# A pool that outlives the head for the second half's first weights, constants and first query block, and a product taken in turn with its transpositions

## The chip, the core and the metric

The kernel runs on one core of a Trainium2 chip. The core has five engines with an instruction queue each: TensorE (PE in the profile, with its weight loads as PEld), VectorE (DVE), ScalarE (ACT), GpSimd (POOL) and SyncE (SP). SP computes nothing here; it issues nearly all DMA transfers, one after the other, and an instruction that has to wait holds up everything behind it on its queue. PE multiplies matrices and also transposes 128 x 128 blocks (a multiplication by the identity, `c_ident`); it writes to PSUM only, and ACT or DVE copy ("evacuate") its results to SBUF. The metric is the time of one execution on the chip, in microseconds (us); less is better. Times of the profile are counted from the start of its span.

## What is computed

One layer of a transformer on 1024 tokens of width 1024, all in float32: a hybrid attention block, a cross attention to a memory of 256 rows, and a squared-ReLU MLP, each with a root-mean-square norm ahead and a residual sum behind. Only the start of the attention block matters here. Cut to that:

```python
proj = h @ w_in                                   # h: normed x, w_in: 1024 x 1760
c_q, c_kv, k_idx, w_idx, q_nsa, kv_nsa, g_nsa = split(proj)
c_q, c_kv = rms_norm(c_q, dsa_cq_g), rms_norm(c_kv, dsa_ckv_g)
q_d = rope(rms_norm(c_q @ w_dsa_uq))              # dense-sparse attention, 8 heads of 64
q_i = rope(c_q @ w_idx_q)                         # indexer: picks 256 keys for each query
q_n = rope(rms_norm(q_nsa))                       # three-branch attention, 8 heads of 64
k_c = rope(rms_norm(compress(kv_nsa[:, :, 0])))   # 63 compressed keys; v_c likewise
...
for each block of 128 queries:
    indexer scores and top 256; attention over them; compressed, selected and window attention
```

## The kernel before

Tokens are worked on in tiles of 128. `project(pool, part, late, st)` (L410) does everything up to queries and keys, for four tiles at a time: part 0 is the head of the program (its pool is `p1`, its PSUM tags D, M and C), part 1 the second half (pool `p2`, opened when `p1` is closed). A part transposes the normed x into `xh` (`to_T`, L294), multiplies it with chunks of 256 columns of `w_in` (`gemm`, L342, whose matmuls all stand at L233), and handles each result in `consume` (L461). In the head the float32 operands are split into a high and a low part (`whi`, `wlo`, L261 and L266: two engines make them from `wraw`); in the second half each weight is used whole and the two tags are only two rings of buffers (`load_whole`, L278). The first chunk is columns 968 to 1224, the raw keys and values of the compressed branch; its result is doubled by ACT (L487), transposed by PE (L490) and copied to `c8` tiles.

The x tiles of the second half are loaded in the head and normed in place by `norm_ahead` (L400). At the start of part 1 they are transposed (eight 128 x 128 blocks a tile, in two PSUM buffers of four, evacuated by ACT at L306 or DVE at L308), and then come, in the code's order, eleven small loads of constants into two `pc` tiles (L437 to L447: gains of norms, and cosine and sine rows that DVE multiplies at L441 and L442), the loads of the first weights, and the first product. At that moment p1 has just been closed, the main PSUM pool has been opened (two buffers for D, one for M, two each for S and PT), and the attention of the first half begins beside part 1: `q_prep` (L613) loads a block of 128 queries by 4 heads from DRAM into `qin` (one buffer), ACT squares it (L627), DVE reduces it (L629), POOL takes the root and normalizes (L630 to L632), POOL and DVE apply the rotation (L633 to L637), and PE transposes it (L643) into a PT buffer. The queries lie in DRAM since the head (`qraw`, written from `st` by `stage_q`, L459).

`together` (L123) and `attend` (L885) interleave attention and the rest in the code; the final order on each engine is made by a scheduler of the framework, which takes the instructions by priority as its own model of time lets them start. A tile in a pool has a tag with a number of buffers; a new tile of the tag waits until an old one is no longer used. With `reuse_waits="tile"` a pool that opens over the memory of a closed one waits tile by tile for what lay there.

Of the kernel before, what the change touches and what calls it, by code (L numbers as in the profile page):

```python
# [9 lines left out]
F32 = mybir.dt.float32  # L10
# [12 lines left out]
P = 128  # L23
# [11 lines left out]
NS = 4  # L35
G = 3
RINGS = {
    "p1": {"x4": 5, "st": 2, "relu": 4, "wraw": 4, "whi": 6, "wlo": 6, "c8": 4, "c4": 2, "kraw": 5, "pc": 2},
    "p2": {"x4": 5, "st": 2, "relu": 2, "whi": 4, "wlo": 4, "c8": 3, "c4": 1, "kraw": 4, "pc": 2},
    "dn": {"b4": 4, "h": 8, "relu": 2, "wraw": 2, "whi": 4, "wlo": 4},  # L40
    "res": {"b4": 4, "g": 2},
    "d2": {"b4": 4, "xo": 2, "h": 8, "relu": 4, "wraw": 6, "whi": 8, "wlo": 8},
# [137 lines left out]
def build(nc, tc, I, C, out):  # L180
# [8 lines left out]
    at = at_pool.__enter__()  # L189
    sp_pool = tc.tile_pool(name="sp", bufs=1, side="right", reuse_waits="tile")  # L190
    srow = sp_pool.__enter__()
    p1_pool, p1_psum = tc.tile_pool(name="p1", bufs=1, reuse_waits="tile"), tc.tile_pool(name="ps1", bufs=1, space=PSUM)
    p1 = p1_pool.__enter__()
    psum.update(pool=p1_psum.__enter__(), n=PSUMS["p1"])
# [205 lines left out]
    def norm_ahead(pool):  # L400

        gb = gain(pool, W["norm1_g"])
        for t in range(4, 8):
# [3 lines left out]
            v.scalar_tensor_tensor(ahead[t], ahead[t], r[:, 0:1], gb, op0=ALU.mult, op1=ALU.mult)  # L407
            yield 1.0

    def project(pool, part, late, st):  # L410
        t0, nt = PARTS[part]
        whole = part > 0
# [9 lines left out]
                load_x(ahead[t], t)  # L422
            begun += list(ws)
        for t in range(nt):
            if whole:
                to_T(pool, ahead.pop(t0 + t), xt_of(t), DM // P, ("M", "D", "D"))
            else:
                norm_T(pool, ahead.pop(t), gb1, xt_of(t))
            yield 1.0
        pe = late["pe"]  # L430
        cq = [ring(pool, "c8", [P, nt, 2, P], F32 if whole else F32R) for _ in xf]
        ckv = [ring(pool, "c4", [P, nt, P], F32 if whole else F32R) for _ in xf]
        kraw = [ring(pool, "kraw", [P, 6, 64]) for t in range(nt)]
        KT = []
        pc = ring(pool, "pc", [P, 512])
        cqg, ckvg, ctab = pc[:, 0:256], pc[:, 256:384], pc[:, 384:512].rearrange("p (a d) -> p a d", d=64)
        nc.sync.dma_start(cqg, row(W["dsa_cq_g"]).to_broadcast([P, 256]))  # L437
        nc.sync.dma_start(ckvg, row(W["dsa_ckv_g"]).to_broadcast([P, 128]))
        nc.sync.dma_start(ctab[:, 0, :], C["c_ccos"])
        nc.sync.dma_start(ctab[:, 1, :], C["c_csin"])  # L440
        v.tensor_tensor(ctab[:, 0, :], ctab[:, 0, :], qg[:, 2, :], op=ALU.mult)  # L441
        v.tensor_tensor(ctab[:, 1, :], ctab[:, 1, :], qgs[:, 2, :], op=ALU.mult)  # L442
        kg = ring(pool, "pc", [P, 8, 64])
        lnb = kg[:, 6, :]
        for h, src in enumerate([W["nsa_kn_g"][1:2], W["nsa_kn_g"][1:2], W["nsa_kn_g"][2:3], W["nsa_kn_g"][2:3],
                                 row(W["dsa_kn_g"]), row(W["idx_k_ln_g"]), row(W["idx_k_ln_b"])]):
            nc.sync.dma_start(kg[:, h, :], src.to_broadcast([P, 64]))  # L447

        qst = []

# [89 lines left out]
        for kv in range(0 if part else 2):  # L540
            p3 = pe[:, kv, :].rearrange("p (a l) -> p a l", a=2)
            g.tensor_copy(KT[kv][0:64, :, nt * P:], p3[0:64])
            g.tensor_copy(KT[kv][64:128, :, nt * P:nt * P + 15], p3[64:128, :, 1:])
        yield from w_in([[(968, 256)]], 4, begun)
        yield from w_in([[(0, 256)], [(256, 200), (1736, 24)]], 0)
        pair_ = (w_in([[(1224, 256)], [(1480, 256)]], 5), compress(pool, part, KT, pe, st, ctab))
        yield from (alternate if part == 0 else chain)(*pair_)
        yield from gemm(pool, [lambda t, k, c=c: c[:, t, :] for c in ckv], 1, nt,
                        W["w_dsa_ukv"], [[(0, 128)]], consume_kv)
        yield from alternate(w_in([[(456, 256)], [(712, 256)]], 2), k_prep())  # L550
        ups = chain(*[gemm(pool, [lambda t, k, c=c: c[:, t, k, :] for c in cq], 2, nt,
                           W[name], [[(0, 256)], [(256, 256)]],
                           lambda ci, t, pt, k=k: stage_q(k, ci, t, pt)) for k, name in ((0, "w_dsa_uq"), (2, "w_idx_q"))])
# [58 lines left out]

    def q_prep(aw, t, kind, hg):  # L613

        q = small(aw, "qin", 256, bufs=1).rearrange("p (h d) -> p h d", d=64)
        part = part_of(t)
        nc.sync.dma_start(q, qraw[kind][part][hg][:, t - PARTS[part][0], :].rearrange("p (h d) -> p h d", d=64))
        ta = small(aw, "qta", 256, bufs=1).rearrange("p (h d) -> p h d", d=64)
        tb = small(aw, "qtb", 256, bufs=1).rearrange("p (h d) -> p h d", d=64)
        if kind == 2:  # L620
            A, B = cos[:, t, None, None, :].to_broadcast([P, 4, 2, 32]), sin[:, t, :]
        else:
            tab = small(aw, "qtab", 128, bufs=1).rearrange("p (a d) -> p a d", d=64)
            g.tensor_tensor(halves(tab[:, 0, :]), halves(qg[:, kind, :]), cos[:, t, None, :].to_broadcast([P, 2, 32]), op=ALU.mult)
            g.tensor_tensor(tab[:, 1, :], sin[:, t, :], qgs[:, kind, :], op=ALU.mult)
            A, B = halves(tab[:, 0, :])[:, None, :, :].to_broadcast([P, 4, 2, 32]), tab[:, 1, :]
            s.activation(ta, q, AF.Square)  # L627
            ss, r = small(aw, "qss", 4), small(aw, "qr", 4)
            v.tensor_reduce(ss, ta, axis=AX.X, op=ALU.add)  # L629
            g.tensor_scalar(ss, ss, 64 * EPS, None, op0=ALU.add)  # L630
            g.tensor_tensor(r, ss, mhalf[:, 0:1].to_broadcast([P, 4]), op=ALU.pow)
            g.tensor_tensor(q, q, r[:, :, None].to_broadcast([P, 4, 64]), op=ALU.mult)  # L632
        g.tensor_tensor(halves(ta), halves(q), A, op=ALU.mult)  # L633
        v.tensor_tensor(halves(tb), swap(q), halves(B)[:, None, :, :].to_broadcast([P, 4, 2, 32]), op=ALU.mult)
        qd = small(aw, "qd", 512, bufs=1).rearrange("p (h b d) -> p h b d", h=4, b=2)
        v.tensor_tensor(qd[:, :, 0, :], ta, tb, op=ALU.add)
        g.tensor_tensor(qd[:, :, 1, :], ta, tb, op=ALU.add)  # L637
        own = ("iqh", "iql", 1) if kind == 2 else ("qh", "ql", 2)
        qh = aw.tile([P, 4, P], F32R, tag=own[0], name=own[0], bufs=own[2])
        ql = aw.tile([P, 4, P], F32R, tag=own[1], name=own[1], bufs=own[2])  # L640
        p2 = pst("PT", [P, 4, P])
        for h in range(4):
            te.transpose(p2[:, h, :], qd[:, h, :, :].rearrange("p b d -> p (b d)"), ident)  # L643
        split_ps(p2, qh, ql)
        return qh, ql
# [683 lines left out]
    def fill():  # L1329
        for part in range(1, len(PARTS)):  # L1330
            with tc.tile_pool(name="p2", bufs=1, reuse_waits="tile") as p2:
                yield from project(p2, part, late, st)
            projected.append(part)
        dn = dn_pool.__enter__()
        yield from memory(dn)
        yield 1, PACES[1]
        yield from between(dn, 0, 2, {}, False)
        yield 3, PACES[2]
        x2s, made = {}, {}
        yield from between(dn, 2, 2, x2s, True, None, lambda: pre_norms(dn, made, x2s))  # L1340
        yield 3, PACES[3]
        yield from mlp(dn, 0, 4, x2s, made)
        yield 5, PACES[4]
        rows = dn.tile([P, 2, 8 * 256], F32, tag="xh", name="xh")
        room = [rows[:, 0, :].rearrange("p (t k n) -> p t k n", t=2, k=8),
                dn.tile([P, 2, 8, 256], F32, tag="xl", name="xl"), rows[:, 1, :].rearrange("p (k n) -> p k n", k=8)]
        yield from between(dn, 4, 2, late["x2s"], False, None, None, room)
# [47 lines left out]
```

## Time and profile before

| | us |
|---|---|
| median of 3 runs | 1745.03 (1742.69 to 1746.1) |
| the profiled execution | 1746.53 |
| its span | 1744.8 |
| mean granted clock of PE over the span | 0.977 of full speed |

The profiled execution is 1.5 us above the median. In the profile's lists a row reads: start, duration, engine, line of the kernel, operation, output<-input, shapes, count, and in brackets how long the engine sat idle before and what ended that. Rows by stretch read: the stretch, its length, busy time and number of instructions of PE, PEld, DVE, ACT and POOL, then PE's granted clock, the share of time in which the 16 DMA engines were busy, and GB/s. Busy shares are means over stages with different limits; what counts is which wait ends last at the place in question.

### The profile page before, as it was taken

How to read it: one execution, taken by the hardware profiler on the slowest of the kernel's cores; microseconds unless marked ns; L12 is line 12 of the kernel's file. 1: busy time of each engine (PE TensorE's matmuls, PEld its weight loads, DVE VectorE, ACT ScalarE, POOL GpSimd, SP SyncE). 2: the span in 40 equal slices, each digit the busy share in tenths (PEclk: the TensorE clock that was granted, in tenths of full speed). 3: DMA queues.
4: the chain of work that ended last, by engine and by line, in shares of the span. 5: the costliest groups of instructions: out<-in, count | busy, mean ns of one | idle time of the engine just before them, and what ended most of it. 6: DMA issues, size and time to landing. Idle time of an engine off the chain costs nothing.

```text
span 1744.8 us, 28298 instructions
## 1 busy us (share of the span) xinstructions
PE 1650.8 (95%) x9390; PEld 1444.2 (83%) x9390; DVE 1006.7 (58%) x2404; ACT 1096.8 (63%) x2749; POOL 938.2 (54%) x1091
## 2 busy tenths in 40 slices
PE   6998998899999998999999999999989899999999
PEld 6997987789878887888888888888878787888888
DVE  4564668767775885666547655555445644333344
ACT  4443796994689689857995589954345554333344
POOL 2354556564552545585676675754153565444455
PEclk9998999999999999999999999999989899999999
DMA  7335222546335312122222122126383444333354
GB/s 206 118 129 121 70 62 70 191 125 174 96 97 182 90 50 64 49 79 73 63 76 78 59 69 74 61 70 224 121 280 99 130 144 122 97 97 97 97 166 136
DMA packets 169521, 192.22 MB, mean 110 GB/s; under 512 B 24608, under 2 KB 134944, under 8 KB 169376
## 3 DMA queue, kind: packets, MB, share of 16 engines
q1 hardware_dynamic: 161296, 179.42, 33.5%
q0 software_dynamic: 7936, 10.49, 2.3%
q8 instruction: 74, 1.21, 0.3%
q14 instruction: 71, 0.58, 0.1%
q10 hardware_dynamic: 144, 0.52, 0.1%
HBM read 172.56 MB, written 17.83 MB: 109 GB/s over the span
## 4 chain that ended last, share of the span: by engine, by line
PE 65%; DVE 9%; POOL 7%; ACT 7%; issue 6%; DMA 5%; SPq 1%; POOLq 0%; ACTq 0%; DVEq 0%
PE psD L233 35%; PE psS L233 16%; PE psM L233 5%; PE psPV L233 4%; PE psPT L753 4%; POOL wlo L266 2%; ACT dmask L697 2%; DMA wraw<-in_w_ff_in_dram 2%; PE psM L302 1%; POOL S L743 1%; ACT S L738 1%; DVE pl L253 1%; DVE S L736 1%; ACT whi L261 1%; PE psPT L643 1%
## 5 line engine op out<-in xcount | busy, mean ns | idle before, releaser
L266 POOL TENSOR_TENSOR wlo<-wraw,whi 128x512 fp32r<-128x512 f32 (+1 forms) x249 | 341.5, 1378 | 251.1 <-ACT whi L261 245.3
L261 ACT ACTIVATE whi<-wraw 128x512 fp32r<-128x512 f32 x369 | 228.3, 627 | 219.2 <-PE psD L233 119.0
L233 PE MATMUL psD<-whi,h 128*128 128x512 f32 x688 | 237.6, 398 | 2.1 <-DVE b L1252 2.0
L266 DVE TENSOR_TENSOR wlo<-wraw,whi 128x512 fp32r<-128x512 f32 (+1 forms) x120 | 125.6, 1049 | 157.5 <-ACT whi L261 120.6
L253 DVE TENSOR_TENSOR pl<-psPT,ph 128x512 fp32r<-128x512 f32 (+1 forms) x232 | 141.8, 620 | 65.4 <-ACT ph L252 64.4
L233 PE MATMUL psD<-wlo,xh 128*128 128x256 f32 (+1 forms) x640 | 176.2, 352 | 1.8 <-DMA wlo<-in_w_in_dram 1.8
L738 ACT ACTIVATE S<-S,mn 128x128 f32<-128x128 f32 (+7 forms) x192 | 142.8, 744 | 54.3 <-DVE mn L736 52.4
L233 PE MATMUL psD<-whi,xh 128*128 128x256 f32 (+1 forms) x640 | 173.8, 351 | 0.9 <-DVE Vd L253 0.9
L252 ACT ACTIVATE ph<-psPT 128x512 fp32r<-128x512 f32 (+1 forms) x232 | 122.4, 540 | 63.8 <-PE psPT L753 55.2
L743 POOL TENSOR_SCALAR S<-S,sums,gi 128x640 f32<-128x640 f32 (+7 forms) x128 | 109.8, 867 | 88.5 <-DVE sums L741 69.5
L233 PEld LDWEIGHTS psD<-whi,h 128*128 128x128 f32 x688 | 129.5, 189 | 28.1 <-DVE b L1252 2.6
L753 PE MATMUL psPT<-c_ident,S 128*128 128x128 f32 x816 | 134.7, 277 | 10.1 <-POOL S L743 3.4
L233 PE MATMUL psD<-wlo,h 128*128 128x512 f32 x344 | 136.9, 399 | 0.1
L233 PEld LDWEIGHTS psD<-wlo,xh 128*128 128x128 f32 x640 | 121.6, 195 | 11.2 <-issue 1.9
L233 PEld LDWEIGHTS psD<-whi,xh 128*128 128x128 f32 x640 | 119.8, 195 | 9.5 <-DVE Vd L253 1.1
L233 PE MATMUL psD<-xh,whi 128*128 128x512 f32 (+1 forms) x352 | 124.1, 353 | 1.0 <-ACT whi L261 1.0
L233 PE MATMUL psD<-xh,wlo 128*128 128x512 f32 (+1 forms) x352 | 122.9, 349 | 0.0
L233 PE MATMUL psD<-xl,whi 128*128 128x512 f32 (+1 forms) x352 | 122.6, 349 | 0.0
L233 PE MATMUL psS<-K,qh 128*128 128x384 f32 (+3 forms) x288 | 111.3, 390 | 8.6 <-ACT ir L665 3.2
L753 PEld LDWEIGHTS psPT<-c_ident,S 128*128 128x128 f32 x816 | 99.1, 142 | 21.9 <-POOL S L743 7.4
L233 PE MATMUL psS<-K,ql 128*128 128x384 f32 (+3 forms) x288 | 97.0, 342 | 0.0
L743 POOL TENSOR_SCALAR S<-S,sums 128x128 f32<-128x128 f32 (+7 forms) x64 | 48.2, 767 | 77.8 <-DVE sums L741 55.2
(333 smaller groups left out, 4577.1 us busy)
## 6 DMA issues: line engine op xcount, KB each, us to landing
wraw<-in_w_ff_in_dram SPq DMA_DIRECT2D x44, 512.0 KB, 4.0
wraw<-in_w_ff_out_dram SPq DMA_DIRECT2D x44, 512.0 KB, 4.1
wraw<-in_w_ff_in_dram SPq DMA_DIRECT2D x64, 256.0 KB, 2.8
wraw<-in_w_ff_out_dram SPq DMA_DIRECT2D x64, 256.0 KB, 2.7
wraw<-in_w_in_dram SPq DMA_DIRECT2D x24, 256.0 KB, 3.6
q<-st SPq DMA_DIRECT2D x12, 512.0 KB, 2.8
qin<-q SPq DMA_DIRECT2D x44, 128.0 KB, 2.4
whi<-in_w_out_dram SPq DMA_DIRECT2D x20, 256.0 KB, 3.4
```

What stands on the lines that cost most here:

```text
L233: te.matmul(o, a, b, start=start, stop=stop)
L252: s.activation(hi, src, AF.Copy)
L253: v.tensor_tensor(lo, src, hi, op=ALU.subtract)
L261: s.activation(hi, raw, AF.Copy)
L266: (v if l == "v" else g).tensor_tensor(lo, raw, hi, op=ALU.subtract)
L302: te.transpose(pt[:, j, :], x_t[:, (c + j) * P:(c + j + 1) * P], ident)
L643: te.transpose(p2[:, h, :], qd[:, h, :, :].rearrange("p b d -> p (b d)"), ident)
L697: s.activation(mask, src, AF.Sign, bias=c, accum_out=over)
L736: v.tensor_tensor_reduce(out=dst, in0=sp, in1=m, scale=1.0, scalar=mn[:, 0:1] if i else 3e38, op0=ALU.add, op1=ALU.min, accum_out=low)
L738: s.activation(S, S, AF.Exp, bias=low, scale=-1.0, accum_out=sums[:, hh:hh + 1])
L743: g.tensor_scalar(Ss[hh], Ss[hh], sums[:, hh:hh + 1], 1.0 if gate is None else gate[:, hh:hh + 1], op0=ALU.mult, op1=ALU.mult)
L753: te.transpose(p2[:, j, hh, :], S[:, (c + j) * P:(c + j + 1) * P], ident)
```

## The change

A new pool `pre` is opened below `p1` and closed only when part 1 is done. Into it the head loads, ahead of its own key preparation, the four weight tiles of the second half's first product (`late["first"]`, 1 MB) and a second set of constants (`late["small"]`; the loads and DVE's two products have become the function `constants`). After the key preparation it loads the first query block (`late["q"]`) from the DRAM buffer that was written just before. `q_prep` uses that tile for the first block, and has two `qin` buffers instead of one for all others. In part 1 the transpositions of tile t+1 now stand, in the code, ahead of the first product's group for tile t, and they alternate over the tags M and D instead of M, D, D. The `pc` tag is gone from p1's and p2's rings.

```diff
+    pre_pool = tc.tile_pool(name="pre", bufs=1, reuse_waits="tile")
+    pre = pre_pool.__enter__()
     p1_pool, p1_psum = tc.tile_pool(name="p1", bufs=1, reuse_waits="tile"), tc.tile_pool(name="ps1", bufs=1, space=PSUM)
...
+    def constants(pool):
+        pc, kg = [pool.tile([P, 512], F32, tag="pc", name="pc", bufs=2) for _ in range(2)]
+        ctab, kg = pc[:, 384:512].rearrange("p (a d) -> p a d", d=64), kg.rearrange("p (a d) -> p a d", d=64)
+        nc.sync.dma_start(pc[:, 0:256], row(W["dsa_cq_g"]).to_broadcast([P, 256]))
+        nc.sync.dma_start(pc[:, 256:384], row(W["dsa_ckv_g"]).to_broadcast([P, 128]))
+        nc.sync.dma_start(ctab[:, 0, :], C["c_ccos"])
+        nc.sync.dma_start(ctab[:, 1, :], C["c_csin"])
+        v.tensor_tensor(ctab[:, 0, :], ctab[:, 0, :], qg[:, 2, :], op=ALU.mult)
+        v.tensor_tensor(ctab[:, 1, :], ctab[:, 1, :], qgs[:, 2, :], op=ALU.mult)
+        for h, src in enumerate([W["nsa_kn_g"][1:2], W["nsa_kn_g"][1:2], W["nsa_kn_g"][2:3], W["nsa_kn_g"][2:3],
+                                 row(W["dsa_kn_g"]), row(W["idx_k_ln_g"]), row(W["idx_k_ln_b"])]):
+            nc.sync.dma_start(kg[:, h, :], src.to_broadcast([P, 64]))
+        return pc, kg
...
         for t in range(nt):
-            if whole:
-                to_T(pool, ahead.pop(t0 + t), xt_of(t), DM // P, ("M", "D", "D"))
-            else:
+            if not whole:
                 norm_T(pool, ahead.pop(t), gb1, xt_of(t))
-            yield 1.0
+                yield 1.0
...
-        pc = ring(pool, "pc", [P, 512])
+        pc, kg = late["small"] if whole else constants(pool)
...
-        yield from w_in([[(968, 256)]], 4, begun)
+        if whole:
+            begun = [[late["first"][k // KG][:, k % KG, :]] for k in range(8)]
+        first = w_in([[(968, 256)]], 4, begun)
+        for t in range(nt if whole else 0):
+            to_T(pool, ahead.pop(t0 + t), xt_of(t), DM // P, ("M", "D"))
+            yield 1.0
+            if t > 0:
+                yield next(first)
+        yield from first
...
+        if not whole:
+            late["first"] = [pre.tile([P, KG, 256], F32, tag="w", name="w", bufs=8 // KG) for _ in range(8 // KG)]
+            for i, w in enumerate(late["first"]):
+                nc.sync.dma_start(w, W["w_in"][i * KG * P:(i + 1) * KG * P, 968:1224].rearrange("(k p) n -> p k n", p=P))
+            late["small"] = constants(pre)
         yield from alternate(w_in([[(456, 256)], [(712, 256)]], 2), k_prep())
+        if not whole:
+            late["q"] = pre.tile([P, 4, 64], F32, tag="q", name="q")
+            nc.sync.dma_start(late["q"], qraw[1][0][0][:, 0, :].rearrange("p (h d) -> p h d", d=64))
...
-        q = small(aw, "qin", 256, bufs=1).rearrange("p (h d) -> p h d", d=64)
         part = part_of(t)
-        nc.sync.dma_start(q, qraw[kind][part][hg][:, t - PARTS[part][0], :].rearrange("p (h d) -> p h d", d=64))
+        if t == 0 and kind == 1 and hg == 0:
+            q = late["q"]
+        else:
+            q = small(aw, "qin", 256).rearrange("p (h d) -> p h d", d=64)
+            nc.sync.dma_start(q, qraw[kind][part][hg][:, t - PARTS[part][0], :].rearrange("p (h d) -> p h d", d=64))
```

On TensorE, right behind the last product of the head, the order before is this (S is a normed x tile, xh its transposed copy, qd a query block, Kc the compressed keys; a row may stand for several equal instructions):

```order
L302 MATMUL psD_1811<-c_ident_74,S_1304 128x128 x4
L302 MATMUL psM_1817<-c_ident_74,S_1304 128x128 x4
L302 MATMUL psD_1893<-c_ident_74,S_1306 128x128 x4
L302 MATMUL psD_1899<-c_ident_74,S_1306 128x128 x4
L302 MATMUL psM_1931<-c_ident_74,S_1308 128x128 x4
L302 MATMUL psD_1937<-c_ident_74,S_1308 128x128 x4
L302 MATMUL psD_1949<-c_ident_74,S_1310 128x128 x4
L302 MATMUL psM_1955<-c_ident_74,S_1310 128x128 x4
L643 MATMUL psPT_1844<-c_ident_74,qd_1839 128x128 x4
L233 MATMUL psS_1851<-Kc_967,qh_1842 128x64
L233 MATMUL psD_2019<-wlo_2011,xh_1810 128x256 x2
```

And in the changed program, at the same place (w is a weight tile of the new pool, relu the doubled first result; lines after L189 have moved):

```order
L304 MATMUL psD_1847<-c_ident_77,S_1330 128x128 x4
L304 MATMUL psM_1853<-c_ident_77,S_1330 128x128 x4
L304 MATMUL psD_1927<-c_ident_77,S_1332 128x128 x4
L235 MATMUL psD_1965<-w_1228,xh_1838 128x256 x2
L235 MATMUL psD_1965<-w_1229,xh_1838 128x256 x2
L304 MATMUL psM_1933<-c_ident_77,S_1332 128x128 x4
L235 MATMUL psD_1965<-w_1230,xh_1838 128x256 x2
L235 MATMUL psD_1965<-w_1231,xh_1838 128x256 x2
L304 MATMUL psD_2052<-c_ident_77,S_1334 128x128 x4
L667 MATMUL psPT_1878<-c_ident_77,qd_1873 128x128 x4
L495 MATMUL psM_1976<-c_ident_77,relu_1974 128x128 x4
L235 MATMUL psD_2087<-w_1228,xh_1838 128x256 x2
```

The product's first group stands behind the third of the eight groups of transpositions instead of behind all eight, the query block behind five of them, and the remaining three groups (rows further down) come between later groups of the product.

On SyncE at the same place (q with numbers is the queries' buffer in DRAM, st its source, pc the constants), before:

```order
L459 DMA q201_87<-st_1772 128x1024
L617 DMA qin_1823<-q100_82 128x256
L437 DMA pc_1994<-in_dsa_cq_g_dram 128x256
L438 DMA pc_1994<-in_dsa_ckv_g_dram 128x128
L439 DMA pc_1994<-in_c_ccos_dram 128x64
L440 DMA pc_1994<-in_c_csin_dram 128x64
L447 DMA pc_2001<-in_nsa_kn_g_dram 128x64 x4
L447 DMA pc_2001<-in_dsa_kn_g_dram 128x64
L447 DMA pc_2001<-in_idx_k_ln_g_dram 128x64
L447 DMA pc_2001<-in_idx_k_ln_b_dram 128x64
L617 DMA qin_1869<-q200_86 128x256
L282 DMA wlo_2011<-in_w_in_dram 128x2x256
```

and in the changed program:

```order
L464 DMA q201_90<-st_1800 128x1024
L641 DMA qin_1903<-q200_89 128x256
L641 DMA qin_2024<-q101_86 128x256
L284 DMA wlo_2435<-in_w_in_dram 128x2x256
L284 DMA whi_2437<-in_w_in_dram 128x2x256
L284 DMA wlo_2439<-in_w_in_dram 128x2x256
L284 DMA whi_2441<-in_w_in_dram 128x2x256
L284 DMA wlo_2897<-in_w_in_dram 128x2x200
```

The first query block, the constants and the first weights are gone from here; two later query blocks and the weights of the second product have moved up behind the last write of the head.

In the middle of the head, VectorE's order (cms and relu belong to the norm of c_q, c8 here to its transposed copy) before:

```order
L471 SCALAR_TENSOR_TENSOR relu_547<-relu_547,cr_552,pc_293 128x256
L253 TENSOR_TENSOR c8_286<-psM_516,c8_285 128x256
L246 TENSOR_SCALAR cms_589<-css_585 128x1
L471 SCALAR_TENSOR_TENSOR relu_586<-relu_586,cr_591,pc_293 128x256
L253 TENSOR_TENSOR c8_286<-psM_555,c8_285 128x256
```

and in the changed program:

```order
L476 SCALAR_TENSOR_TENSOR relu_550<-relu_550,cr_555,pc_296 128x256
L255 TENSOR_TENSOR c8_289<-psM_519,c8_288 128x256
L420 TENSOR_TENSOR pc_1236<-pc_1236,qg_263 128x64
L421 TENSOR_TENSOR pc_1236<-pc_1236,qgs_268 128x64
L248 TENSOR_SCALAR cms_592<-css_588 128x1
L476 SCALAR_TENSOR_TENSOR relu_589<-relu_589,cr_594,pc_296 128x256
L255 TENSOR_TENSOR c8_289<-psM_558,c8_288 128x256
```

The two products on the second half's constants stand between the evacuation and the next tile's statistics. On SyncE the four weight loads of the new pool stand between the second and the third of the head's four weight tiles of columns 256 to 456, and the eleven constants behind four further weight tiles.

More of the change, by code (lines that the diff above doesn't have):

```diff
@@ L37 @@
 RINGS = {
-    "p1": {"x4": 5, "st": 2, "relu": 4, "wraw": 4, "whi": 6, "wlo": 6, "c8": 4, "c4": 2, "kraw": 5, "pc": 2},
-    "p2": {"x4": 5, "st": 2, "relu": 2, "whi": 4, "wlo": 4, "c8": 3, "c4": 1, "kraw": 4, "pc": 2},
+    "p1": {"x4": 5, "st": 2, "relu": 4, "wraw": 4, "whi": 6, "wlo": 6, "c8": 4, "c4": 2, "kraw": 5},
+    "p2": {"x4": 5, "st": 2, "relu": 2, "whi": 4, "wlo": 4, "c8": 3, "c4": 1, "kraw": 4},
     "dn": {"b4": 4, "h": 8, "relu": 2, "wraw": 2, "whi": 4, "wlo": 4},
@@ L434, in project @@
         KT = []
-        pc = ring(pool, "pc", [P, 512])
+        pc, kg = late["small"] if whole else constants(pool)
         cqg, ckvg, ctab = pc[:, 0:256], pc[:, 256:384], pc[:, 384:512].rearrange("p (a d) -> p a d", d=64)
[L437 to L443, printed above, removed]
         lnb = kg[:, 6, :]
-        for h, src in enumerate([W["nsa_kn_g"][1:2], W["nsa_kn_g"][1:2], W["nsa_kn_g"][2:3], W["nsa_kn_g"][2:3],
-                                 row(W["dsa_kn_g"]), row(W["idx_k_ln_g"]), row(W["idx_k_ln_b"])]):
-            nc.sync.dma_start(kg[:, h, :], src.to_broadcast([P, 64]))
         qst = []
@@ L1333, in fill @@
             projected.append(part)
+        pre_pool.__exit__(None, None, None)
         dn = dn_pool.__enter__()
```

## The prediction

> **What bounds the kernel now.** I read the head of the page and its chain of work first, then busy time by stretch, then the instructions of the stretch that stood out. The first rows are the page's span, its busy time and the chain by engine.
>
> ```profile
> span 1744.8 us, 28298 instructions
> PE 1650.8 (95%) x9390; PEld 1444.2 (83%) x9390; DVE 1006.7 (58%) x2404; ACT 1096.8 (63%) x2749; POOL 938.2 (54%) x1091
> PE 65%; DVE 9%; POOL 7%; ACT 7%; issue 6%; DMA 5%; SPq 1%; POOLq 0%; ACTq 0%; DVEq 0%
> ```
>
> TensorE (PE) is busy for 95% and carries 65% of the chain, so the end moves by what PE idles or loses to a lower clock. The next view gives each engine's busy time where the first half's projection ends and the second half's begins (then PE's clock, DMA share and GB/s).
>
> ```profile
> 125.00:130.00 5.00, 4.29 (x38) 3.93 (x37) 4.32 (x11) 1.90 (x4) 0.00 (x0) 1.00 0.32 129
> 130.00:135.00 5.00, 1.02 (x8) 0.55 (x6) 1.62 (x4) 1.39 (x3) 2.32 (x4) 0.82 0.45 117
> 135.00:140.00 5.00, 1.54 (x5) 1.00 (x5) 1.15 (x4) 0.60 (x1) 1.83 (x4) 0.50 0.48 115
> 140.00:145.00 5.00, 4.07 (x12) 3.35 (x12) 1.82 (x4) 0.42 (x1) 1.94 (x2) 0.50 0.96 297
> 145.00:150.00 5.00, 5.00 (x22) 4.22 (x23) 2.21 (x10) 1.73 (x6) 4.62 (x7) 0.81 1.14 227
> ```
>
> PE is idle for 0.71 + 3.98 + 3.46 + 0.93 = 9.1 us of these 25, and from 133 to 147 it has half its clock: 0.1 + 1.54 + 4.07 + about 1.9 us busy there, so about 3.7 us more are lost. **12.8 us** stand open in this stretch. PE's own rows, with idle time and its releaser in brackets, say what it waits for; the page's queue rows say why.
>
> ```profile
> 126.12 0.60 PE L302 MATMUL psD<-c_ident,S 128*128 128x128 f32 x4
> 132.44 0.66 PE L302 MATMUL psM<-c_ident,S 128*128 128x128 f32 x4 [2.07 <-ACT xh L306]
> 136.89 1.12 PE L643 MATMUL psPT<-c_ident,qd 128*128 128x128 f32 x4 [3.79 <-POOL qd L637]
> 140.93 3.75 PE L233 MATMUL psD<-wlo,xh 128*128 128x256 f32 x8 [1.82 <-DMA wlo<-in_w_in_dram]
> 152.80 1.03 PE L233 MATMUL psD<-wlo,xh 128*128 128x256 f32 x4
> 153.67 1.03 PE L233 MATMUL psD<-whi,xh 128*128 128x256 f32 x4
> ```
>
> ```profile
> 101.19 0.34 SPq L459 DMA_DIRECT2D q<-st  x1
> 113.13 0.34 SPq L459 DMA_DIRECT2D q<-st  x1
> 117.83 10.74 SPq L459 DMA_DIRECT2D q<-st  x4
> 128.66 0.38 SPq L617 DMA_DIRECT2D qin<-q  x1
> 129.10 0.78 SPq L437 DMA_DIRECT2D pc<-in_dsa_cq_g_dram  x1
> 136.16 0.44 SPq L282 DMA_DIRECT2D wlo<-in_w_in_dram  x1
> ```
>
> The queue comes free at 128.6, issues the first query block, eleven constants (from 129.10) and, behind a second query block, the first weights (136.16). The first product starts at 140.93, 14.8 us after the first transposition; the second starts at 152.80. At full clock four of its matmuls cost 0.87 us (152.80 to 153.67).
>
> **The change, part by part.** *Weights and constants.* The four loads and eleven constants leave the queue at this place, so PE's wait for DMA (1.82) goes, and the second product's weights follow the query blocks, from about 129.5 instead of 141.6. The first query block is now loaded on the queue behind the write of it at 101.19; that load waits until the write has landed, and the next write it could hold up is issued only at 113.13, so this is free. What is late next is the query block and its chain. The rows of it before, and the evacuations ahead of it:
>
> ```profile
> 126.81 0.60 ACT L306 ACTIVATE xh<-psD 128x512 f32<-128x512 f32 x1
> 128.10 0.68 DVE L308 COPY xh<-psM 128x512 f32<-128x512 f32 x1
> 131.49 0.42 ACT L627 ACTIVATE qta<-qin 128x256 f32<-128x256 f32 x1 [3.26 <-DMA qin<-q]
> 131.94 0.42 DVE L629 TENSOR_REDUCE qss<-qta 128x4 f32<-128x256 f32 x1 [2.52 <-ACT qta L627]
> 132.77 1.04 POOL L631 TENSOR_TENSOR qr<-qss,mhalf 128x4 f32<-128x4 f32 x1
> 133.89 0.61 POOL L632 TENSOR_TENSOR qin<-qin,qr 128x256 f32<-128x256 f32 x1
> 134.40 0.23 DVE L441 TENSOR_TENSOR pc<-pc,qg 128x64 f32<-128x64 f32 x1 [1.45 <-DMA pc<-in_c_ccos_dram]
> 135.87 0.97 POOL L637 TENSOR_TENSOR qd<-qta,qtb 128x256 f32<-128x256 f32 x1 [0.56 <-DVE qtb L634]
> 140.22 0.97 POOL L633 TENSOR_TENSOR qta<-qin,c_cos 128x256 f32<-128x256 f32 x1 [2.83 <-DMA qin<-q]
> ```
>
> I keep the clock of before and walk the new order. Three groups of transpositions run from 126.12 to 127.4; the product's first four matmuls follow the evacuation at 126.81 + 0.60 and end at 128.3. The next group needs DVE's evacuation, which stays behind DVE's old work and ends at 128.78: **0.5 us** of wait. That group, the other four matmuls and one more group last to 130.6. Now PE stands at the transpositions of the first query block. Its data lies in memory since the head, ACT squares it at 127.3, but DVE takes the reduction only after that evacuation, at 128.8. From reduction to transposition the rows before took 136.89 - 131.94 = 4.95 us, of them about 0.5 behind the constants' two products on DVE (134.40), which are gone: ready at 128.8 + 4.4 = 133.2. **2.6 us** of wait, where before there were 2.07 and 3.79.
>
> *The following query blocks.* Behind the first block PE has 8.0 us of work up to the transposition of the first compressed scores: 20 product matmuls at 0.87 / 4 (4.3), six groups of transpositions at 0.43 (2.6; three groups fill 126.12 to 127.4), eight score matmuls (1.1, an estimate from these). The data of those rows comes from POOL, one block behind the other: 133.2, + 2.6 (second block, 0.97 + 0.97, and 0.6 for two short tables, estimated from 0.97 for 256 columns), + 1.0 (hand-over to the third over ACT and DVE, 0.42 each), + 4.1 (third: 1.04 + 0.61 + 0.97 + 0.97, and about 0.5 of small steps), + 1.6 (tables and the fourth's first step), + 1.2 (scaling the compressed scores, estimated as above) = 143.7. PE waits 143.7 - 133.2 - 8.0 = 2.5, and about 0.3 for one more evacuation: **2.8 us**. Below it could be zero, if PE's work lies more evenly than I think; above, 4.5, one further chain of 4.1 and a hand-over. The second product then starts at about 145.4 instead of 152.8. Waits that stay: 0.5 + 2.6 + 2.8 = 5.9.
>
> *The clock.* Before, four half-clock windows of 3.4 us covered 133.2 to 146.9. Whether a pause costs one is read where the program idled less:
>
> ```profile
> 488.20:491.60 3.40, 1.51 (x9) 1.03 (x9) 1.17 (x4) 1.99 (x7) 3.40 (x5) 1.00 0.00 0
> 491.60:495.00 3.40, 3.15 (x13) 2.52 (x13) 2.79 (x8) 3.30 (x9) 1.73 (x4) 0.50 0.01 2
> 150.00:800.00 650.00, 610.94 (x3457) 534.96 (x3456) 451.55 (x1315) 502.29 (x1465) 358.01 (x506) 0.97 0.33 98
> 800.00:1250.00 450.00, 446.76 (x2392) 381.51 (x2392) 257.51 (x584) 319.50 (x709) 275.58 (x273) 1.00 0.27 86
> ```
>
> A window 44% busy was followed by windows at 0.50. The pause of 2.6 us can make such a window, so up to 1.7 us (half of 3.4) may go, most of it ahead of waits for POOL that would be there anyway. I take **0.5**, ends 0 and 1.7. The Trainium skill (TensorE: Matmul & The Clock Gate, Part 1: The HAM clock gate) has the clock fall after an idle window of about 3.4 us. By that rule a pause of 2.6 us costs nothing and the sum gains 0.5; the trace disagrees as the rule is worded, since 1.51 us of work stood in the window before a fall.
>
> *The head.* Two products on the constants now stand in DVE's order behind the row at 42.34, and wait for tables that are queued behind 1 MB of weights.
>
> ```profile
> 34.96 24.31 SPq L271 DMA_DIRECT2D wraw<-in_w_in_dram  x12
> 35.00:41.00 6.00, 4.37 (x37) 4.17 (x36) 3.01 (x8) 3.99 (x13) 1.69 (x2) 1.00 0.88 211
> 41.00:47.00 6.00, 6.00 (x53) 6.00 (x52) 3.24 (x7) 3.78 (x12) 2.64 (x4) 1.00 0.03 10
> 42.34 0.43 DVE L253 TENSOR_TENSOR c<-psM,c 128x256 fp32r<-128x256 f32 x1
> 44.04 0.15 DVE L246 TENSOR_SCALAR cms<-css 128x1 f32<-128x1 f32 x1 [1.28 <-ACT relu L468]
> 44.92 1.42 DVE L471 SCALAR_TENSOR_TENSOR relu<-relu,cr,pc 128x256 f32<-128x256 f32 x1 [0.73 <-POOL cr L248]
> 47.48 0.38 PE L302 MATMUL psM<-c_ident,relu 128*128 128x128 f32 x2
> ```
>
> The DMA engines were 0.88 busy at 211 GB/s to 41, then empty. 1.05 MB more is 5 us, so they run to about 46, and the tables land between 46.0 and 48.5; I take 47.4. DVE's statistics (44.04) then come at 47.65, the row (44.92 - 44.04 later, 0.48 undisturbed) ends at 49.0, and PE's transpositions (47.48) wait **1.6 us**; ends 0.2 and 2.7. Queued behind DVE's wait, and behind POOL's wait for it, stand the root of the same row and two weight splits, late by as much; PE reaches them later than the transpositions. The weights' 1 MB itself falls into the empty 41 to 47. The Trainium skill (DMA: Bandwidth & Descriptors, Anatomy of one DMA, there for the GpSimd path) gives a DMA a fixed 2.0 us and bytes / 436e9. By these the estimate is 2.4 us for the 1 MB and tables landed by about 44, so no wait of PE and 1.6 us more gain. The row above, on SyncE's queue, shows 211 GB/s, half that rate, and decides.
>
> *The query double buffer.* PE's waits after 150 name no query load, so I cost it at nothing; what it can hide is the 2.83 us wait on POOL (140.22), which is off PE's path later.
>
> **The sum.** 12.8 - 5.9 - 0.5 - 1.6 = 4.8 us. The profiled execution took 1746.53 (its span 1744.8 and 1.7 around it), so 1741.7; the median of the runs shown is 1.5 lower, 1745.03, and gives **1740.2**. It reaches the end because from 800 on PE is filled to over 99% (446.8 of 450 us to 1250) and its rows stand in one order in both kernels from seven tenths of the program on. Over 0.2% (3.5 us) is what a measurement of this kernel tells from no change.
>
> **Rivals.**
> *The new bound eats it* (the head's stall, POOL's chain and a clock window at their upper ends): 12.8 - (0.5 + 2.6 + 4.5) - 1.7 - 2.7 = 0.8 us, 1744; at half of these surpluses 1742.5. For it: POOL has no gap from 132 on. Against: three upper ends at once. No change. 0.24.
> *The lead grows*: the second query block's transposition comes at 136.4 instead of 146.8, and ACT and DVE carry the attention beside the projection to 350. With no clock window and no head stall the stretch gives 6.9, and 3 us of the 39 that PE idles from 150 to 800 (650 - 610.94) follow: 1735. 0.17.
> *Slower, by the clock between 150 and 800.* The order of PE is mixed there by up to ten rows. A mean clock of 0.97 over 650 us is about 11 half-clock windows, 1.7 us each when filled. Small pauses that move together would add windows; from five more on (8.5 us) the gain is turned into 3.7 us of loss, 1748.7. For it: windows at 44% fall. Against: PE's work stands at the same places within those ten rows, and pauses may as well part. 0.14.
> *The change doesn't do what it says*: the scheduler could have left the product behind the transpositions. The rows shown with the change have it between them, so this gets no chance.
>
> **How the numbers follow.** The forecast has 0.45, alone 1737.5 to 1743, three quarters of it faster and the rest within 0.2%. Faster: 0.34 + 0.17 = 0.51; same: 0.11 + 0.24 = 0.35; slower 0.14. The range 1732 to 1748 leaves out less than 2 in 10: the slower case and the tip of the best.
>
> **What would show it.** Right: first product's matmuls between 127 and 129, second product near 145 + 1.6, PE's longest wait of the stretch on the query block's rows, one half-clock window at most, DVE waiting for the tables near 43 to 47. Wrong: a wait for weights still there; a PE wait in the head over 3 us; idle time between 150 and 800 far from 39 us.

## The result, and the profile after

| | before | changed |
|---|---|---|
| median of 4 runs, us | 1745.57 (1742.69 to 1747.11) | 1726.78 (1725.02 to 1728.59) |
| profiled execution, us | 1746.53 | 1728.59 |
| its span, us | 1744.8 | 1726.8 |

The ratio is 0.9894 with an interval of 0.9877 to 0.9911: 18.8 us faster, where 4.8 had been forecast and the range ended 5 us above the time found. All medians are of executions at the usual clock; one execution each of e1, e3 and the kernel before ran at a mean granted clock of 0.84, 0.75 and 0.56 and is left out.

The page of the changed kernel has the same busy time but for the clock: PE's instructions are the same 9390, and their busy time fell by 7.7 us.

```profile
span 1726.8 us, 28309 instructions
PE 1643.1 (95%) x9390; PEld 1437.8 (83%) x9390; DVE 1007.5 (58%) x2404; ACT 1092.9 (63%) x2749; POOL 946.0 (55%) x1091
PE 67%; DVE 5%; ACT 5%; DMA 2%; POOL 2%; issue 2%; SPq 0%; ACTq 0%; DVEq 0%; POOLq 0%
```

The span is thus 10.3 us of PE's idle time and 7.7 us of half clock shorter. Since both kernels have the same number of PE records, the span can be cut at the same record in both. For each stretch the table gives PE's idle time plus half of its busy time at half clock, worked out from all records; both kernels were profiled a second time (runs e9 and e10 below), and e1, e8, e12 and e11 are experiments. The changed kernel, e10, e1, e8 and e12 have the same order of PE's rows. Stretches are named by their times before.

| us lost | before | again | changed | again | e1 | e8 | e12 | e11 |
|---|---|---|---|---|---|---|---|---|
| head, 0 to 60 | 13.3 | 14.5 | 17.2 | 16.7 | 14.3 | 14.1 | 13.4 | 13.9 |
| 115 to 165 (the transition) | 13.1 | 11.3 | 1.5 | 1.7 | 1.5 | 1.5 | 1.5 | 2.1 |
| 165 to 800 | 57.2 | 55.5 | 47.5 | 48.5 | 51.6 | 47.4 | 44.2 | 56.6 |
| 800 to 1195 | 3.2 | 5.2 | 1.2 | 1.2 | 1.2 | 1.2 | 1.5 | 7.8 |
| 1195 to the end | 36.9 | 40.7 | 38.1 | 35.8 | 38.3 | 36.7 | 37.9 | 40.2 |

From 60 to 115 every run loses 0.9 or 1.0. Between the first two profiles the transition gives 11.6, the stretch to 800 gives 9.7, the next one 2.0; the head takes 3.9 and the end 1.2.

The transition first, busy time by stretch as before (PE, PEld, DVE, ACT, POOL, then clock, DMA share, GB/s):

```profile
125.00:130.00 5.00, 4.86 (x41) 4.65 (x40) 4.90 (x9) 2.73 (x7) 1.63 (x4) 1.00 0.52 210
130.00:135.00 5.00, 5.00 (x33) 4.48 (x32) 3.69 (x10) 1.79 (x4) 1.69 (x3) 1.00 0.40 131
135.00:140.00 5.00, 3.61 (x23) 3.08 (x22) 2.59 (x6) 2.14 (x5) 4.54 (x7) 1.00 1.01 305
140.00:145.00 5.00, 5.00 (x33) 4.55 (x32) 2.98 (x11) 2.95 (x9) 3.90 (x6) 1.00 0.73 174
145.00:150.00 5.00, 5.00 (x30) 4.50 (x29) 3.12 (x9) 1.60 (x6) 2.04 (x5) 1.00 0.81 190
```

The clock stays full, and the one gap is that of 135 to 140. PE's rows from the first transposition to the second product show it and what lies around it:

```profile
130.02 0.60 PE L304 MATMUL psD<-c_ident,S 128*128 128x128 f32 x4
131.37 1.99 PE L235 MATMUL psD<-w,xh 128*128 128x256 f32 x8
133.20 0.60 PE L304 MATMUL psM<-c_ident,S 128*128 128x128 f32 x4
133.63 1.89 PE L235 MATMUL psD<-w,xh 128*128 128x256 f32 x8
137.35 0.66 PE L667 MATMUL psPT<-c_ident,qd 128*128 128x128 f32 x4 [1.39 <-POOL qd L661]
138.28 3.62 PE L235 MATMUL psD<-w,xh 128*128 128x256 f32 x16
143.44 3.62 PE L235 MATMUL psD<-w,xh 128*128 128x256 f32 x16
149.65 0.38 PE L837 MATMUL psPT<-c_ident,cS 128*128 128x128 f32 x2
150.88 1.03 PE L235 MATMUL psD<-wlo,xh 128*128 128x256 f32 x4
```

PE waits 1.39 us for the first query block and then for nothing: the compressed scores' transposition (149.65), for which a wait of 2.5 us had been worked out, finds its data ready. The second product starts 20.9 us behind the first transposition, before 26.7.

In the head, rows of VectorE, then of SyncE's queue, then of PE, and the stretch behind:

```profile
42.86 0.43 DVE L255 TENSOR_TENSOR c<-psM,c 128x256 fp32r<-128x256 f32 x1
47.35 0.23 DVE L420 TENSOR_TENSOR pc<-pc,qg 128x64 f32<-128x64 f32 x1 [4.06 <-DMA pc<-in_c_ccos_dram]
47.65 0.15 DVE L248 TENSOR_SCALAR cms<-css 128x1 f32<-128x1 f32 x1
36.48 2.16 SPq L566 DMA_DIRECT2D w<-in_w_in_dram  x4
43.68 0.97 SPq L418 DMA_DIRECT2D pc<-in_c_ccos_dram  x1
50.01 0.41 PE L304 MATMUL psM<-c_ident,relu 128*128 128x128 f32 x2 [1.84 <-DVE relu L476]
50.00:55.00 5.00, 4.99 (x30) 5.00 (x31) 3.96 (x12) 0.92 (x4) 2.41 (x3) 0.66 0.73 205
```

VectorE stands for 4.06 us at the first of its two products on the constants, until the table lands at 47.35; PE then waits 1.84 us, and the clock falls for one window of 3.4 us behind it.

### The profile page after: what moved, and what is told of

It is laid out like the page before. It is cut to its first block, busy times and chain, and to the rows that moved or that the text cites. A ratio compares the mean times of both kernels' runs of the same rounds, so it can differ in the third digit from the quotient of the medians.

```text
span 1726.8 us, 28309 instructions
## 1 busy us (share of the span) xinstructions
PE 1643.1 (95%) x9390; PEld 1437.8 (83%) x9390; DVE 1007.5 (58%) x2404; ACT 1092.9 (63%) x2749; POOL 946.0 (55%) x1091
## 4 chain that ended last, share of the span: by engine, by line
PE 67%; DVE 5%; ACT 5%; DMA 2%; POOL 2%; issue 2%; SPq 0%; ACTq 0%; DVEq 0%; POOLq 0%
PE psD L235 33%; PE psS L235 17%; PE psM L235 7%; PE psPV L235 4%; PE psPT L777 4%; ACT dmask L721 1%; DMA wraw<-in_w_ff_in_dram 1%; POOL wlo L268 1%; ACT S L762 1%; PE psPT L667 1%; DVE pl L255 1%; PE psM L304 1%; ACT ph L254 1%; ACT whi L263 1%; DVE S L760 1%
## 5 line engine op out<-in xcount | busy, mean ns | idle before, releaser
L268 POOL TENSOR_TENSOR wlo<-wraw,whi 128x512 fp32r<-128x512 f32 (+1 forms) x249 | 345.1, 1393 | 250.3 <-ACT whi L263 245.9
L762 ACT ACTIVATE S<-S,mn 128x128 f32<-128x128 f32 (+7 forms) x192 | 142.6, 744 | 52.3 <-DVE mn L760 51.6
L235 PE MATMUL psD<-whi,xh 128*128 128x256 f32 (+1 forms) x608 | 166.2, 349 | 1.2 <-DVE Vd L255 1.1
L235 PE MATMUL psD<-wlo,xh 128*128 128x256 f32 (+1 forms) x608 | 166.0, 348 | 0.0
L235 PEld LDWEIGHTS psD<-wlo,xh 128*128 128x128 f32 x608 | 114.7, 194 | 8.3
L235 PEld LDWEIGHTS psD<-whi,xh 128*128 128x128 f32 x608 | 113.6, 194 | 9.0 <-DVE Vd L255 1.5
L721 ACT ACTIVATE dmask<-tkh,tkt 128x384 bf16<-128x384 uint16 (+5 forms) x96 | 84.2, 877 | 6.2 <-DVE tkl L705 4.9
```

The source lines that it names most:

```text
L235: te.matmul(o, a, b, start=start, stop=stop)
L268: (v if l == "v" else g).tensor_tensor(lo, raw, hi, op=ALU.subtract)
L721: s.activation(mask, src, AF.Sign, bias=c, accum_out=over)
L762: s.activation(S, S, AF.Exp, bias=low, scale=-1.0, accum_out=sums[:, hh:hh + 1])
```

## The experiments

All were timed beside runs of the kernel before on the same chip; a ratio is to those. "Lost" is idle time plus half-clock loss as in the table.

**e1: the constants' loads moved in the code behind the query columns.**

```diff
-            late["small"] = constants(pre)
         yield from alternate(w_in([[(456, 256)], [(712, 256)]], 2), k_prep())
         if not whole:
+            late["small"] = constants(pre)
             late["q"] = pre.tile([P, 4, 64], F32, tag="q", name="q")
```

> The changed kernel with the second constants' loads (and so DVE's two products) moved in the code behind the projections of the query columns; SyncE's order stays, VectorE has the two products two normalizations later, at the place that before ran near 47 us. Theory 'the head pays for the tables' (a stall of 1.84 us on PE near 50 us and a half-clock window behind it, 1.71 us): the stall and the window go, about 3.5 us faster than the changed kernel, 1723 us. Rival 'the head's loss is the transfers' (1 MB more beside the head's own loads): nothing moves, 1727 us.

The median was 1727.13, ratio 0.9891 (0.9872 to 0.9910): as the change. But the edit moved nothing that runs. The scheduler gave PE, VectorE, ACT, POOL and SyncE's loads the changed kernel's order, row by row, and VectorE and PE still wait at the same places:

```profile
45.70 0.22 DVE L420 TENSOR_TENSOR pc<-pc,qg 128x64 f32<-128x64 f32 x1 [3.46 <-DMA pc<-in_c_ccos_dram]
48.38 0.41 PE L304 MATMUL psM<-c_ident,relu 128*128 128x128 f32 x2 [1.25 <-DVE relu L476]
```

So this run tests neither theory; it is a third profile of the change. PE's pause came out shorter (1.25 us instead of 1.84 and, in e10, 1.85) and no half-clock window followed it, so 14.3 us are lost to 60 us instead of 17.2. From 165 to 800 us it loses 51.6.

**e8: the constants loaded ahead of the weights** (the two statements of `late["small"]` and `late["first"]` exchanged).

> The changed kernel with the eleven constants loaded ahead of the 1 MB of weights: PE's order is that of the changed kernel row by row. Theory 'the tables' landing decides the head': VectorE's products run by 43 us, no wait of PE near 50 us and no window behind it, 115 us is reached 3 us earlier. What lies between 165 and 800 us then shows how much two executions of one order differ there: by up to 5 us of half-clock loss if the windows fall by chance, under 1 us if they belong to the order. Time 1724 to 1728 us.

1723.89 us, ratio 0.9870 (0.9851 to 0.9889), 2.9 us below the change. VectorE has the table at 39.53, and PE is filled where the change had its stall:

```profile
39.53 0.23 DVE L420 TENSOR_TENSOR pc<-pc,qg 128x64 f32<-128x64 f32 x1 [0.84 <-DMA pc<-in_c_ccos_dram]
45.00:50.00 5.00, 5.00 (x47) 5.00 (x45) 4.09 (x7) 3.37 (x11) 3.73 (x3) 1.00 0.80 240
50.00:55.00 5.00, 5.00 (x47) 5.00 (x46) 3.93 (x18) 1.75 (x9) 1.10 (x2) 1.00 0.64 211
```

The same 1 MB of weights is now issued from 43.66 on, lands by 51.3 (in the change by 43.0) and costs PE nothing, so the head's loss was the tables' place in the queue. From 165 to 800 it loses 47.4, with PE's order that of the change row by row; what other runs with this order lost there stands under e12.

**e5: weights and constants in the new pool, nothing else.**

> The changed kernel with the weights and constants in the new pool and nothing else: first query block from the queue, one query buffer, all transpositions ahead of the product with tags M, D, D. Theory 'weights and constants alone fill the transition, the query chain costs a few us behind': the first product follows the transpositions without a wait for DMA, PE idles 3 to 5 us between 125 and 160 us instead of 9.1 us, 1736 us. Rival 'without the early query block PE stands as before': 8 us idle, 1742 us.

1736.22 us, ratio 0.9939 (0.9920 to 0.9958). PE waits 0.72 and 2.08 us at the transpositions and has one half-clock window; the transition loses 4.6 instead of 13.1. The loads alone are worth 8.5 of the 11.6 us gained there.

**e6: no early query block** (it comes from the queue like all others).

> The changed kernel with the first query block loaded from the queue behind the head's last write, as all others; two query buffers, weights, constants and the turn by turn order stay. Theory 'the early query block saves its landing': PE waits about 3 us for the first block and may take a half-clock window, 1730 us. Rival 'the order puts product work in its place': no wait over 1 us, 1727 us.

1728.81 us, ratio 0.9902 (0.9883 to 0.9920). The transition loses 2.0. PE waits 1.1 us for an evacuation by VectorE and never for the block: the early load is worth about half a microsecond there (the change loses 1.5 to 1.7). The mechanism is the rival's, the time lies between the two.

**e2: all transpositions ahead of the product again, tags M, D, D.**

```diff
-        first = w_in([[(968, 256)]], 4, begun)
         for t in range(nt if whole else 0):
-            to_T(pool, ahead.pop(t0 + t), xt_of(t), DM // P, ("M", "D"))
+            to_T(pool, ahead.pop(t0 + t), xt_of(t), DM // P, ("M", "D", "D"))
             yield 1.0
-            if t > 0:
-                yield next(first)
-        yield from first
+        yield from w_in([[(968, 256)]], 4, begun)
```

> The changed kernel with the eight groups of transpositions ahead of the product again, tags M, D, D; weights, constants, first query block and two query buffers stay as changed. Theory 'the turn by turn order fills the evacuations' waits': PE idles about 3 to 4 us again between 130 and 145 us and may take one half-clock window, 1731 us. Rival 'the loads were all of it': within 2 us of the changed kernel, 1727 us.

1734.82 us, ratio 0.9938 (0.9916 to 0.9959): nearer the time of my theory, but not for its reason. PE's rows in this kernel:

```profile
130.26 0.66 PE L304 MATMUL psM<-c_ident,S 128*128 128x128 f32 x4 [0.74 <-DVE tkt L709]
131.72 0.60 PE L304 MATMUL psM<-c_ident,S 128*128 128x128 f32 x4
132.15 6.29 PE L235 MATMUL psD<-w,xh 128*128 128x256 f32 x28
138.28 0.60 PE L664 MATMUL psPT<-c_ident,qd 128*128 128x128 f32 x4
```

One wait of 0.74 us among the transpositions, and then 28 records of the product (14 matmuls, by the count given further down) in one row, behind which the query block is ready: the transition loses 0.9, less than the change's 1.5. Taking product and transpositions in turn gains nothing at the place where it stands. Its profile, taken from an execution 3.2 us above the median, loses 53.6 and 7.6 us in the two stretches behind 165 us, the change's three profiles 47.5 to 51.6 and 1.2: the loss lies there.

**e3: the change with one query buffer** (`bufs=1` in `qin`).

> The changed kernel with one buffer for the query blocks behind the first, as before. Theory 'the second buffer is worth nothing' (no PE wait names a query load): 1727 us, within 2 us. Rival 'the second buffer feeds the attention from 165 to 800 us, where 8 us of the gain lie': 1735 us, with the half-clock windows of this stretch back.

1731.32 us, ratio 0.9919 (0.9901 to 0.9937), 4.5 above the change. PE's order is the same through the transition, and the loss is there, 6.3 instead of 1.5. Rows of SyncE's queue, ACT and PE in this kernel:

```profile
137.76 0.56 SPq L641 DMA_DIRECT2D qin<-q  x1
142.62 0.42 ACT L651 ACTIVATE qta<-qin 128x256 f32<-128x256 f32 x1 [5.01 <-DMA qin<-q]
142.94 0.58 ACT L492 ACTIVATE relu<-psD 128x512 f32<-128x512 f32 x1
143.57 5.41 PE L235 MATMUL psD<-w,xh 128*128 128x256 f32 x16 [3.01 <-ACT relu L492]
```

With one buffer the third block's load waits for the second block, and the scheduler has put it behind the weights of the second product: it is issued at 137.76 (in the change from 132.58 on with the second), though the second block's last reader, on POOL, is done at 135.68. ACT stands 5.01 us at the square of that block; queued behind it is the evacuation of the product's result (L492), and PE waits 3.01 us for that, with a half-clock window behind. In the profile's waits this has ACT's name, not that of a query load.

**e4: the kernel before with two query buffers.**

> The kernel before with two buffers for the query blocks and nothing else. Theory 'worth nothing': 1745 us, within 2 us. Rival 'it feeds the attention from 165 to 800 us': 1737 us, with the transition at 130 us as before.

1738.90 us, ratio 0.9955 (0.9938 to 0.9972), so the rival's size, but its place is wrong: the transition loses 11.5 (before 13.1 and 11.3), 165 to 800 loses 55.0, 800 to 1195 1.2. All stretches of its profile lose 120.5, against 124.8 in the first profile of before; of a span that is 7.8 us shorter, 3.5 are not placed.

**e7: the kernel before with the tags M, D.**

> The kernel before with the second half's transpositions over the tags M, D instead of M, D, D and nothing else: no load, buffer or wait of the change is in it, yet the order of the attention behind it is another in thousands of rows. Theory 'part of the gain behind 165 us is the order that the scheduler happens to give': the transition stays at 9 us idle and four half-clock windows, and the sum of idle time and half-clock loss from 165 to 1250 us moves by 3 us or more either way from the 57 and 3 us of before. Rival 'that stretch gains only by the change's own loads and buffers': within 2 us there, 1745 us.

1742.11 us, ratio 0.9973 (0.9960 to 0.9986). The transition loses 11.4, 165 to 800 53.9, 800 to 1195 1.9. An edit that adds no load and no buffer gains 4 us, spread over stretches that it doesn't name.

**e9: the kernel before again. e10: the change again.**

> The kernel before, profiled a second time. Theory 'the stretch from 165 to 800 us belongs to the order, its half-clock windows within one or two': idle time and half-clock loss there within 3 us of the 57.3 us of the first profile. Rival 'the windows fall by chance': 52 us or less, and the 9.8 us between the first profiles of before and of the change is in good part chance.

> The changed kernel, profiled and timed a second time beside the next two. Theory 'belongs to the order': idle time and half-clock loss from 165 to 800 us within 3 us of 47.5 us, 1726.8 us. Rival 'chance': 51 us or more.

The second profiles lose 55.5 (before, 1748.57 us) and 48.5 (change, median 1726.48, ratio 0.9888 with 0.9868 to 0.9908) from 165 to 800: within 2 us of the first ones, as the first theory of both had it. But e1, which is the change a third time, lost 51.6 there, which is what the rival of e10 had named. Two profiles were too few to tell.

**e11: e8 with the tags M, D, D**, still in turn with the product.

> The kernel with the constants loaded ahead of the weights (e8), its transpositions taken in turn with the product over the tags M, D, D instead of M, D: all loads, buffers and the turn by turn order stay, the order of the attention behind is another in thousands of rows. Theory 'half of the gain is the order that the scheduler happens to give': the transition stays under 2 us of waits, the stretch from 165 to 1250 us loses 3 us or more against e8, 1728 to 1732 us. Rival 'the change's own parts hold that gain': within 2 us of e8, 1724 us.

1736.82 us, ratio 0.9956 (0.9939 to 0.9973), 12.9 above e8, more than either theory had, and as much above e12, which was timed beside it. The executions don't overlap (1734.59 to 1743.83, those of e8 and e12 1720.28 to 1726.23). The transition still loses only 2.1. The profiled execution is the slowest of nine, 7.0 us above the median, so its rows show more loss than is usual for this kernel. Busy time of e8 (first two rows) and of e11 from 150 to 800 and from 800 to 1250 us:

```profile
150.00:800.00 650.00, 612.49 (x3493) 534.04 (x3492) 463.19 (x1331) 509.76 (x1483) 368.89 (x510) 0.98 0.31 98
800.00:1250.00 450.00, 441.54 (x2384) 378.26 (x2383) 258.59 (x583) 313.93 (x704) 277.15 (x274) 1.00 0.29 94
```

```profile
150.00:800.00 650.00, 612.72 (x3458) 535.01 (x3458) 459.05 (x1321) 504.71 (x1464) 366.09 (x503) 0.97 0.31 96
800.00:1250.00 450.00, 443.94 (x2373) 378.75 (x2372) 251.45 (x572) 316.32 (x702) 278.08 (x272) 1.00 0.27 88
```

In this execution PE is as busy in both, yet e8 gets 35 instructions more done by 800 us: at half clock e11 loses 19.3 us from 165 to 800, e8 9.9, with 37.3 and 37.5 us idle (the same stretch by records). More half-clock windows hardly explain the median, though: five of the other executions had a mean clock of 0.982 or 0.983, against 0.984 in e8, and still took 1734.59 to 1737.75 us. Over the whole span the profile of e11 has 6.8 us more idle time than e8's, 4.9 of them from 800 to 1195 us. Where the rest of the 12.9 us lies in a usual execution is not shown.

**e12: e8 with three query buffers.**

> The kernel with the constants loaded ahead of the weights (e8) and three buffers for the query blocks; PE's order is the same row by row. Theory 'two buffers cover the chain of a query block': 1724 us, within 1 us of e8. Rival 'each further buffer feeds the attention earlier': 1720 us.

1723.94 us, ratio 0.9871 (0.9850 to 0.9891): as e8, so two buffers cover the chain. e8 and e12 are the best versions of the study.

Five profiles now have one order of PE's rows: the change, e10, e1, e8 and e12. From 165 to 800 us their idle time is 35.5 to 37.5 us, and their half-clock loss 8.5 to 15.3 us, with 6 to 10 windows. So the idle time there repeats within 2 us; the windows that it sets off do not.

## Why the prediction was wrong, step by step

*What bounds the kernel, and the 12.8 us open in the transition:* right. The transition lost 13.1 us before by all records.

*Weights, constants and first query block:* right in direction and place. PE's wait for DMA went, the first product stands between the third and fourth group of transpositions, the second product follows without a wait for its weights.

***Waits that stay, 5.9 us*: this step failed; 1.5 to 1.7 was measured.** The working counted the product's matmuls by rows of the instruction order (4 + 4 ahead of the first query block, 20 behind it) and priced them by records of the trace: 0.87 us for four. But a matmul of plain float32 leaves two records. The order has four matmuls with w at the place where the trace has 131.37 with x8, and 32 in all where the trace has 64. So 28 matmuls cost 12.2 us and not 6.1. With that, the same walk gives: PE reaches the query block 1.74 us later and waits 2.6 - 1.74 = 0.9 (measured 1.39); behind it PE has 8.0 + 4.35 = 12.4 us of work against 10.5 of POOL's chains, so no wait (measured none); and the evacuation by VectorE (0.5) is covered by the longer product. POOL's chain itself was sized well. Its last rows in the change are these:

```profile
145.44 0.72 POOL L657 TENSOR_TENSOR qta<-qin,c_cos 128x256 f32<-128x256 f32 x1
146.91 0.88 POOL L830 TENSOR_SCALAR cS<-cS,csum,gi 128x128 f32<-128x128 f32 x2 [0.75 <-DVE csum L827]
```

From the first block's transposition at 137.35 to the end of the scaling at 147.8 are 10.4 us, where 10.5 had been worked out.

*The clock, 0.5:* no window fell in the transition, as the lower end had it.

*The query double buffer at nothing:* wrong, 4.8 us in the transition (e3, 6.3 against 1.5). I looked for PE waits with the name of a query load; the load holds up ACT, and PE waits for what is queued behind it on ACT.

*The head, 1.6:* the mechanism and the stall were right (tables at 47.35, forecast 47.4; PE's wait 1.84, 1.85 and 1.25 in the change's three profiles). The half-clock window behind it, 1.7 us more in two of the three, was not priced, though the same rule was used for the transition. Seven profiles have this pause (those three, e2, e3, e5 and e6): the window of 3.41 us in which most of it fell was 46 and 49% busy in the two where the clock fell, and 56 to 73% in the other five.

***What lies behind 150 us at nothing*: this step failed too, and was the larger miss, 8 to 12 us.** From 165 to 1195 us the two profiles of before lose 60.4 and 60.7 us, the change's three 48.7, 49.7 and 52.8. The working put nothing there, on the ground that PE's waits name no query load and that PE's work stands at the same places. Two things changed. From 165 to 800 the idle time fell from 39.1 and 39.7 us to between 35.5 and 37.5: about the 3 us that the rival "the lead grows" had put there. And fewer half-clock windows fell: 11 and 10 before, 7, 9 and 10 in the change; the slower rival had this mechanism with the other sign.

Part of it is the order that the scheduler makes. When only the tags of eight groups of transpositions differ, the median moves by 12.9 us (e8 and e11) or by 4 (before and e7), and the transition by no more than 2. The kernels of the change with M, D, D (e2, e11) lie at 1734.8 and 1736.8, near what the parts of the change earn by themselves: 1745.6 less the 11.6 of the transition, and with the head's 3 to 4 where they are paid, makes 1734 to 1737.5. The other 8 to 10 us come with M, D beside these loads. That the tags do it by the order alone is argued from the unchanged transition, not shown: no run kept the tags and changed only the order. Part of it is chance, as the five profiles of one order show. Why that order waits less is not settled; nothing was tried that would show it.

## What to carry to other kernels

Check the unit of a count before it is priced: find one place where the order and the trace show the same instructions, and divide. Look in the trace whether an edit of the code moved the instructions at all; e1's did not. When an edit lets a scheduler re-order thousands of rows, time a control that re-orders as much and changes nothing else (other tags, another place in the code); here such a control moved the time by 4 and by 13 us, as much as the edit's own parts. Profile one program more than twice before a stretch is said to repeat, and see where the profiled execution lies among the others. A load that comes late, for want of a buffer or by its place in the queue, shows itself as a wait on the engine whose queue holds its first reader, so look up what stands behind that reader.

## What the runs showed of the hardware

**When the clock falls and comes back.** The granted clock changes on a grid of 3.41 us whose phase differs between most of the profiles. Cutting the fourteen profiles on their grids: of 125 full-clock windows with PE busy for under half, 122 were followed by one at half clock; between 50 and 70% 29 of 183; between 70 and 75% 4 of 83; above, none of 6353. To come back it needs more work than it takes to stay: of 103 half-clock windows with PE busy under 80%, all were followed by another; from 80 to 90% 17 of 24; above 90% 6 of 154. So a pause that empties over half a window mostly costs 1.7 us more, half of the next one if that is filled, and a shorter pause seldom does. The Trainium skill (TensorE: Matmul & The Clock Gate, Part 1: The HAM clock gate) has the fall after at least one idle window and a free-running window; the second agrees with the phases, the first is too mild by these counts, since windows with up to half of their time busy were followed by a fall.

**A float32 matmul.** Rows of the change, the first two of the head's split operands (fp32r, one record per matmul), the third of plain float32:

```profile
125.80 0.28 PE L235 MATMUL psD<-wlo,c 128*128 128x256 f32 x1
125.92 0.40 PE L235 MATMUL psD<-whi,c 128*128 128x256 f32 x2
150.88 1.03 PE L235 MATMUL psD<-wlo,xh 128*128 128x256 f32 x4
```

A split one of 256 columns takes 0.12 us (125.80 to 125.92); a record of the float32 kind 0.22 (0.87 for four) and a matmul, with two of them, 0.43 us. The Trainium skill (FP8 and Floating Point Precision, TensorE Precision Notes) has float32 in four passes; 0.43 to 0.12, or 3.6, is near that.
